# One transformer block, attention loop: GpSimd's stores, loads, table steps and splits in units of their own, and keys split over all tokens

## The chip, the cores and the metric

One core of a Trainium2 chip runs the whole program. The metric is device time in microseconds. The profile counts from the first to the last instruction (the span); the time of an execution is a little longer than its span. The engines are TensorE (PE, with its weight loads PEld), VectorE (DVE), ScalarE (ACT), GpSimd (POOL) and SyncE (SP, which issues transfers).

## The reference, cut to what matters

One layer of a diffusion backbone over 1024 latent tokens and 256 context tokens, width 1024, in float32. Tokens are normalised and modulated, projected, mixed by a pooling mixer (half the width) and by neighbourhood attention (8 heads of 64), projected out, and sent through a squared-ReLU MLP. The part that the change touches is the attention:

```python
s_loc = einsum('bnqhd,brnkhd->bhnqrk', q_r, k_b) * scale      # keys of the window
s_loc = where(col_mask, s_loc + bias, -inf)                    # learned 2-D position bias
s_ctx = einsum('bnqhd,bkhd->bhnqk', q_r, k_ctx) * scale        # all 256 context keys
p = softmax(concatenate([s_loc, s_ctx]))
o = p_loc @ v_b + p_ctx @ v_ctx
```

The latent grid has 16 rows of 64 columns. Each query sees a window of 8 rows by 16 columns and all context keys. After it come `mix @ w_out`, a gate row (`gt1`), the residual, and the second modulation (`sc2`, `sh2`).

## The kernel before, in words

**Three passes.** A float32 product is made of three products on rounded parts. A "split" makes them: `hi` is a cast of the source to the rounded type, `lo = src - hi`; then `hi*hi + hi*lo + lo*hi` is accumulated. A split of 128x512 is two instructions. `split` (L156) casts on ScalarE (L146) and subtracts on VectorE (L152). In the attention `high` (L1112) casts on ScalarE and puts the subtraction into the list `lows`, which `low()` empties on VectorE. `parts_of` with an engine (L901, L902) does both on GpSimd.

**Units.** Tokens are regrouped into 8 bands of 8 columns (128 tokens each). The attention runs over 32 units: 4 pairs of heads `j`, 8 bands `m` each. A unit's 128 queries see three bands of local keys (m-1, m, m+1) and the context; the bands 0 and 7 see two. A software pipeline runs over units, `for i in range(N + 4)` with N = 32. Iteration i does, among others:

- `weighed(i - 4)`: the weighted output of unit i-4 into the head page `heads[j]` (VectorE);
- `scores(i)` (L991): scores of both heads on TensorE into PSUM `S`; then on VectorE the bias table is added and the minimum `nm` found (L1027); between the two heads `share(i - 1)`: reciprocal of the sums `ri` on VectorE (L1042) and its copy over 128 columns `rb` on GpSimd (L1044);
- `turn(i - 2)`: TensorE transposes `rb` and the probabilities (L1057); `fifth_kept`: ScalarE copies them (`px`, L1071); `turn_kept`: ScalarE and VectorE copy the rest (`pt`, L1076);
- `exps(i, e)`: exponentials and sums on ScalarE (L1038);
- `values(i - 3)`: probabilities times values on TensorE (`pa`, L1091).

There are two `S` buffers, one for each head, so the scores of unit i+1 wait for VectorE's pass over unit i. Two output products of the query projection, `last_query("P4", i)`, stand in iterations 0 and 1. In iterations 32 to 35 the first products of the output projection (`pox`) take the scores' place.

**Order.** `in_order` ties each engine's instructions to the order in which the program writes them, for TensorE, ScalarE, VectorE and SyncE in the loop and for GpSimd through `first_pool`. An instruction that waits holds up everything behind it on its engine.

**What else stands in the loop.** Each of these is placed by hand at an iteration:

- bias tables: `tables(j)` (L867) loads the raw table of head pair j (SyncE) and then subtracts it from the mask in four steps of three GpSimd instructions (L884). There are two table pairs; j uses pair `j % 2`. Before, one step is taken at the top of each iteration from m = 1 on.
- splits of keys and queries: each half of 512 tokens of a head pair is split by itself, so `keys[j, b]` has b = 0, 1. The units m = 3 and m = 4 see bands of both halves, and their local scores are computed in two pieces.
- modulation rows: the gate row "a" and the rows "sc" and "sh" are summed over partitions by eight small matmuls (L236), copied or gated, stored to DRAM by four DMAs of GpSimd (`mod_out`, L253), and "sc" and "sh" are loaded back as columns (L623). `column_sums` (L620) does all of that in one go, at iterations 5 and 8; row "a" is gated and stored at iteration 4. All stand ahead of `scores(i)`, so ahead of `rb` on GpSimd.
- accumulating DMAs of GpSimd (`add_to`, L187): second halves of the heads at i = 3 mod 8 (from 11), first halves at i = 15, 23, 31.
- the output projection's weights: `weight_load` at the iterations in `LOADS` (SyncE), `weight_split(n)` at those in `HALVES`; `mixed_split(j)`, the split of the finished head page's first half, at iterations 8, 16, 24 and 32.

**Memory.** Most tiles are pages of 128x1024 from a pool of 33 (`page`); eight more tiles of that size lie in the pool `whl` (called `small` or `spare` below). A tile takes a buffer when one is free; whoever writes it first waits until the last reader of the buffer's former tile is done.

Of the kernel before, what the change touches and what calls it, by code (L numbers as in the profile page):

```python
# [18 lines left out]
P = 128  # L19
# [61 lines left out]
def hybrid_block(ctx, tc, x, ctx_in, w_mod, b_mod, gp1, gp2, w_in, pool_w, rpb, w_out, w1, w2, vectors,  # L81
# [189 lines left out]
    with tc.tile_pool(name="ps1", bufs=6, space=PSUM) as ps1, tc.tile_pool(name="tmp1", bufs=3) as tmp:  # L271
# [348 lines left out]
        def column_sums(name, acc, to, bank):  # L620
            nc.scalar.copy(acc[:, :256], mod_sums_of(name, acc, bank))
            mod_out(name, acc)
            nc.gpsimd.dma_start(to, gates[name].rearrange("o (k p) -> p (o k)", p=P))  # L623
# [267 lines left out]
        keys, queries, kcs = {}, {}, []  # L891

        def parts_of(to, j, b, small=False, engine=None):
            name = f"{'k' if to is keys else 'q'}P{j}_{b}"
            src = kT[j][:, b * 512 : (b + 1) * 512] if to is keys else qT[j][b]
            t = whl.tile([P, 1024], F32R, tag="hl", name=name) if small else page(name, F32R)
            hi, lo = to[j, b] = t[:, :512], t[:, 512:]
            if engine is None:
                split(src, hi, lo)
            else:  # L900
                engine.tensor_copy(hi, src)  # L901
                engine.tensor_tensor(lo, src, hi.bitcast(F32), sub)  # L902
# [42 lines left out]
        with in_order(ET.PE, ET.Pool, ET.Activation, ET.DVE, ET.SP) as pooling:  # L945
            banks = {of: [bank(f"p{of}{j}") for j in range(2)] for of in "KQ"}
            use(-1)
            for step, (n, of, j) in enumerate([(n, of, j) for n, of in products for j in range(2)]):
# [23 lines left out]
                if step == 20:  # L972
                    parts_of(keys, 0, 0)
                if step == 22:
                    parts_of(queries, 0, 0, True)


    with (
# [12 lines left out]
        def scores(i):  # L991
# [4 lines left out]
            q = queries[j, m // 4]  # L996
# [4 lines left out]
            t0, t1 = (m - 1, m + 2) if inner else (m + o - 1, m + o + 1)  # L1001
            at = 128 if inner else 256
# [37 lines left out]
        def share(i):  # L1040
# [3 lines left out]
            nc.gpsimd.tensor_copy(shares[i].rearrange("p (e t) -> p e t", e=2),  # L1044
                                  ri.rearrange("p (e o) -> p e o", o=1).to_broadcast([P, 2, HD]))
# [74 lines left out]
        def mixed_split(j):  # L1120
            mp = mix["A12"][j] = page(f"mix0_{4 + j}", F32R)
            high(heads[j][:, :512], mp[:, :512], mp[:, 512:])

        def weight_split(n):
# [911 lines left out]
```

## Time and profile before

| | us |
|---|---|
| time, median of 3 runs | 1037.98 |
| lowest and highest | 1036.62, 1038.22 |
| profiled execution, its own time | 1037.68 |
| span of that execution | 1035.9 |
| mean granted TensorE clock | 0.995 |
| attention loop's scores, first and last start | 218.95, 324.81 |

The profile is read by stage: TensorE's busy time in a stretch, and where it is idle, which engine's instruction released it. Busy time of TensorE is modelled, so the starts of successive units are a better measure of a unit's length than busy time is. Engines off the path may be idle at no cost.

### The profile page before, as it was taken

The page shows a single profiled execution, that of the slowest core. Times are in us where ns is not written, and L with a number is a line of the kernel's source. Part 1 is how long each engine was busy: PE and PEld are TensorE (multiplying, and loading weights), DVE is VectorE, ACT ScalarE, POOL GpSimd, SP SyncE. Part 2 cuts the span into 40 slices and gives each one's busy share as a digit, 9 for nine tenths or more (in the row PEclk, how much of TensorE's full clock was granted, in tenths as well). Part 3 has the DMA queues.
Part 4 walks back from the last instruction along what each step waited for, and adds up shares of the span by engine and source line. Part 5 has one row for each costly group of instructions (what it writes and reads, how often), then busy time and mean ns, then how long its engine had stood idle before and what let it go on. Part 6 is the DMA issues. An engine that isn't in the chain of part 4 may idle for free.

```text
span 1035.9 us, 16106 instructions
## 1 busy us (share of the span) xinstructions
PE 1015.6 (98%) x5958; PEld 842.6 (81%) x5958; DVE 752.6 (73%) x1165; ACT 549.0 (53%) x951; POOL 133.0 (13%) x214
## 2 busy tenths in 40 slices
PE   8999999998999999999999999999999999999997
PEld 6788888876888888888888888888888888888885
DVE  5588757875886598878998888755766666547576
ACT  7573255355898556876655544555543334334431
POOL 3011200245732312310000000000000000000001
PEclk9999999998999999999999999999999999999999
DMA  9999798542338786794786666536967766656556
GB/s 342 330 257 333 255 265 282 203 102 63 73 74 214 175 193 193 231 265 165 250 274 208 221 199 229 203 112 240 324 230 268 246 226 220 203 175 195 171 182 212
DMA packets 123134, 222.71 MB, mean 215 GB/s; under 512 B 9456, under 2 KB 55152, under 8 KB 123056
## 3 DMA queue, kind: packets, MB, share of 16 engines
q1 hardware_dynamic: 96560, 171.14, 50.5%
q0 software_dynamic: 9360, 19.58, 9.3%
q10 hardware_dynamic: 17136, 30.97, 8.0%
q8 instruction: 47, 0.77, 0.3%
q14 instruction: 31, 0.25, 0.1%
HBM read 168.16 MB, written 52.45 MB: 213 GB/s over the span
## 4 chain that ended last, share of the span: by engine, by line
PE 73%; ACT 1%; issue 1%; DVE 0%; POOL 0%; DMA 0%; POOLq 0%; DVEq 0%; ACTq 0%
PE phz L198 3%; PE phv L198 3%; PE phx L198 3%; PE pyx L198 3%; PE pa L1091 3%; PE phx L199 3%; PE pyx L200 3%; PE phx L200 3%; PE pyv L199 3%; PE phz L200 3%; PE pyz L199 3%; PE pyx L199 3%; PE phv L200 3%; PE pyz L198 3%; PE pyv L198 3%; PE phv L199 3%
## 5 line engine op out<-in xcount | busy, mean ns | idle before, releaser
L1038 ACT ACTIVATE sp<-sp,nm 128x640 f32<-128x640 f32 (+1 forms) x64 | 51.6, 806 | 9.3 <-DVE ri L1042 4.5
L1622 ACT ACTIVATE c<-c 128x512 f32<-128x512 f32 x48 | 30.3, 632 | 44.3 <-DVE c L1742 25.1
L1027 DVE CUSTOM_DVE_ANT_0 sp<-S,tab 128x640 f32<-128x640 f32 (+1 forms) x56 | 44.5, 794 | 12.7 <-PE pz L1057 6.8
L146 ACT CAST wpS<-S 128x512 fp32r<-128x512 f32 x64 | 38.7, 616 | 28.1 <-PE phv L200 10.1
L198 PE MATMUL phx<-thB,wpA 128*128 128x512 f32 x128 | 50.2, 392 | 0.0
L199 PE MATMUL phx<-tlB,wpA 128*128 128x512 f32 x128 | 49.9, 390 | 0.0
L200 PE MATMUL phx<-thB,wpA 128*128 128x512 f32 x128 | 49.9, 389 | 0.0
L152 DVE TENSOR_TENSOR wpS<-S,wpS 128x512 fp32r<-128x512 f32 x64 | 43.4, 686 | 8.2 <-ACT wpS L146 8.2
L140 POOL TENSOR_TENSOR ry<-vy,nhalf 128x1 f32<-128x1 f32 x8 | 5.9, 740 | 280.7 <-DVE vy L138 280.7
L1623 ACT ACTIVATE c<-c 128x512 f32<-128x512 f32 x48 | 30.2, 630 | 14.4 <-DVE sa L1705 13.6
L1076 DVE COPY pt<-T 128x512 f32<-128x512 f32 x32 | 22.0, 687 | 9.7 <-PE T L1057 6.8
L198 PEld LDWEIGHTS phx<-thB,wpA 128*128 128x128 f32 x128 | 24.0, 188 | 5.5 <-ACT s L1673 0.5
L1091 PE MATMUL pa<-pt,v 128*64 128x128 f32 x352 | 26.5, 285 | 1.6 <-ACT px L1071 1.4
L200 PEld LDWEIGHTS phx<-thB,wpA 128*128 128x128 f32 x128 | 24.0, 188 | 5.0
L199 PEld LDWEIGHTS phx<-tlB,wpA 128*128 128x128 f32 x128 | 24.1, 188 | 4.8
L1012 PE MATMUL S<-kP,qP 64*128 64x256 f32 (+2 forms) x240 | 25.8, 324 | 0.9 <-DVE nm L1027 0.9
L198 PE MATMUL phz<-thB,wpS 128*128 128x512 f32 x64 | 25.0, 391 | 0.0
L198 PE MATMUL phv<-thT,wpA 128*128 128x512 f32 x64 | 25.0, 391 | 0.0
L200 PE MATMUL phz<-thB,wpS 128*128 128x512 f32 x64 | 24.9, 390 | 0.0
L199 PE MATMUL phv<-tlT,wpA 128*128 128x512 f32 x64 | 24.9, 389 | 0.0
L199 PE MATMUL phy<-tlT,wpS 128*128 128x512 f32 x64 | 24.9, 389 | 0.0
L198 PE MATMUL phz<-thT,wpS 128*128 128x512 f32 x64 | 24.9, 389 | 0.0
(1112 smaller groups left out, 3419.2 us busy)
## 6 DMA issues: line engine op xcount, KB each, us to landing
b<-in_w SPq DMA_DIRECT2D x64, 512.0 KB, 4.4
hrS<-hdS SPq DMA_DIRECT2D x32, 512.0 KB, 5.1
hrA<-hdA SPq DMA_DIRECT2D x24, 512.0 KB, 5.5
wm<-in_w_mod SPq DMA_DIRECT2D x16, 512.0 KB, 9.8
wa_0w<-in_w SPq DMA_DIRECT2D x16, 512.0 KB, 4.8
wa_1w<-in_w SPq DMA_DIRECT2D x16, 512.0 KB, 4.5
hdA<-c ACTq DMA_DIRECT2D x32, 256.0 KB, 2.7
hdS<-sa ACTq DMA_DIRECT2D x32, 256.0 KB, 2.4
```

The source lines that it names most:

```text
L146: nc.scalar.copy(hi, src)
L152: nc.vector.tensor_tensor(lo, src, hi.bitcast(F32), sub)
L198: nc.tensor.matmul(ps, ahi, bhi, start=first, stop=False, skip_group_check=more)
L199: nc.tensor.matmul(ps, ahi, blo, start=False, stop=False, skip_group_check=more)
L200: nc.tensor.matmul(ps, alo, bhi, start=False, stop=last, skip_group_check=more)
L1012: nc.tensor.matmul(S[e][:, c0 : c0 + k[0].shape[1]], q[n_q][hs, cols], k[n_k][hs], start=(n_q + n_k == 0), stop=(n_q == 1))
L1027: nc.vector.tensor_tensor_reduce(out=to, in0=s, in1=bt, scale=1.0, scalar=BIG, op0=add, op1=ALU.min, accum_out=nm)
L1038: nc.scalar.activation(sp, sp, AF.Exp, bias=least[i, e], scale=-1.0, accum_out=sums[i][:, e : e + 1])
L1076: copy(turns[i].rearrange("p e i t -> p (e i) t")[:, :, h * HD : (h + 1) * HD], turned[i][h].rearrange("p (a t) -> p a t", a=8))
L1091: nc.tensor.matmul(pa[e * HD : (e + 1) * HD, cols], v[:, f : f + HD], turns[i][:, e, c] if c < 4 else fifths[i][:, :, (e + 1) * HD : (e + ...
L1622: nc.scalar.activation(r, src, AF.Relu)
L1623: nc.scalar.activation(r, r, AF.Square)
```

## The change

GpSimd's other work in the loop is written as a table `jobs`, which names for an iteration what is issued right behind `scores(i)`, so behind that iteration's `rb`.

- `column_sums` only sums and copies; the store (`out_of`) and the load as a column (`columns_of`) become jobs: row "a" stored in unit 5, "sc" stored in 6 and loaded in 10, "sh" stored in 9 and loaded in 12.
- Table steps (`built`) become jobs: pair 1 in units 0 to 4, pair 2 in 9, 10, 12, 13 (two steps), pair 3 in 18, 20 (two), 21 (two). The first of each only loads.
- `mixed_split` of head pairs 0 to 2 and the first four weight halves go from ScalarE and VectorE to GpSimd: units 8, 16, 24 and 26, 28, 29, 30 (before: 8, 16, 24 and 12, 14, 20, 22). The weight loads move from 8, 16 to 16, 20.
- Keys are split into one `hi` and one `lo` tile over all 1024 tokens of a head pair (`key_parts`), so that every unit takes its local keys as one slice. The halves are still written one by one. The second half of pair 2 goes from GpSimd (iteration 7) to ScalarE and VectorE (unit 0). GpSimd's other splits of keys and queries move from 6, 8, 9, 14, 15, 16 to 7, 14, 17, 18, 22, 25. Which tiles lie in pages and which in `whl` changes.
- The last unit's `rb` copy goes from GpSimd to VectorE.

```diff
-        def column_sums(name, acc, to, bank):
+        def column_sums(name, acc, bank):
             nc.scalar.copy(acc[:, :256], mod_sums_of(name, acc, bank))
-            mod_out(name, acc)
+
+        def columns_of(name, to):
             nc.gpsimd.dma_start(to, gates[name].rearrange("o (k p) -> p (o k)", p=P))
...
-        keys, queries, kcs = {}, {}, []
+        kparts, qparts, kcs = [None] * 4, {}, []
+
+        def apart(src, hi, lo, pool):
+            if pool:
+                nc.gpsimd.tensor_copy(hi, src)
+                nc.gpsimd.tensor_tensor(lo, src, hi.bitcast(F32), sub)
+            else:
                 split(src, hi, lo)
+
+        def part_page(name, spare):
+            return whl.tile([P, 1024], F32R, tag="hl", name=name) if spare else page(name, F32R)
+
+        def key_parts(j, b, spare=False, pool=False):
+            if kparts[j] is None:
+                kparts[j] = [part_page(f"kP{j}{n}", spare) for n in "hl"]
+            bs = slice(b * 512, b * 512 + 512)
+            apart(kT[j][:, bs], kparts[j][0][:, bs], kparts[j][1][:, bs], pool)
+
+        def query_parts(j, b, spare=False, pool=False):
+            t = part_page(f"qP{j}_{b}", spare)
+            qparts[j, b] = t[:, :512], t[:, 512:]
+            apart(qT[j][b], *qparts[j, b], pool)
...
                 if step == 20:
-                    parts_of(keys, 0, 0)
+                    key_parts(0, 0)
                 if step == 22:
-                    parts_of(queries, 0, 0, True)
+                    query_parts(0, 0, True)
...
-            local = []
-            for b in range(2):
-                b0, b1 = max(t0, 4 * b), min(t1, 4 * b + 4)
-                if b0 < b1:
-                    local.append((at + (b0 - t0) * P, [a[:, (b0 - 4 * b) * P : (b1 - 4 * b) * P] for a in keys[j, b]]))
-            parts = local + [(512, ck)] if inner else [(0, ck)] + local
+            ts = slice((m - 1) * P, (m + 2) * P) if inner else slice((m + o - 1) * P, (m + o + 1) * P)
+            local = [a[:, ts] for a in kparts[j]]
+            parts = ((128, local), (512, ck)) if inner else ((0, ck), (256, local))
...
-            nc.gpsimd.tensor_copy(shares[i].rearrange("p (e t) -> p e t", e=2),
-                                  ri.rearrange("p (e o) -> p e o", o=1).to_broadcast([P, 2, HD]))
+            (nc.gpsimd if i < N - 1 else nc.vector).tensor_copy(
+                shares[i].rearrange("p (e t) -> p e t", e=2),
+                ri.rearrange("p (e o) -> p e o", o=1).to_broadcast([P, 2, HD]))
...
-        LOADS, HALVES = (8, 16, 26, 28), (12, 14, 20, 22, 32, 33, 33, 34)
+        LOADS, HALVES = (16, 20, 26, 28), (None, None, None, None, 32, 33, 33, 34)
...
-        def high(src, hi, lo):
+        def high(src, hi, lo, pool=False):
+            if pool:
+                apart(src, hi, lo, True)
+                return
             nc.scalar.copy(hi, src)
             lows.append(lambda: nc.vector.tensor_tensor(lo, src, hi.bitcast(F32), sub))
...
-            early_parts = [(keys, 0, 1, True), (keys, 1, 0, True), (queries, 1, 0, True), (keys, 1, 1),
-                           (keys, 2, 0, True), (queries, 2, 0, True)]
-            for p in early_parts[:3]:
-                parts_of(*p)
-            for j in range(2):
-                last_query("P7", j)
-                for p in early_parts[3 + 2 * j : 5 + 2 * j]:
-                    parts_of(*p)
-            parts_at = {1: (queries, 0, 1)}
-            parts_at.update({i: (to, j, b, j == 2, nc.gpsimd) for i, to, j, b in
-                             ((6, queries, 1, 1), (7, keys, 2, 1), (8, queries, 2, 1), (9, keys, 3, 0),
-                              (14, keys, 3, 1), (15, queries, 3, 0), (16, queries, 3, 1))})
-            coming_tables = iter(())
+            key_parts(0, 1)
+            key_parts(1, 0, True)
+            query_parts(1, 0, True)
+            last_query("P7", 0)
+            key_parts(1, 1)
+            last_query("P7", 1)
+            key_parts(2, 0, True)
+            query_parts(2, 0)
+
+            table = [None] + [tables(j) for j in (1, 2, 3)]
+            built = lambda j: next(table[j])
+            out_of = lambda n: mod_out(n, accs[n])
+            jobs = {0: [(built, 1), (key_parts, 2, 1)], 1: [(built, 1)], 2: [(built, 1)], 3: [(built, 1)], 4: [(built, 1)],
+                    5: [(out_of, "a")], 6: [(out_of, "sc")], 7: [(query_parts, 1, 1, True, True)],
+                    8: [(mixed_split, 0, True)], 9: [(built, 2), (out_of, "sh")],
+                    10: [(columns_of, "sc", scale2), (built, 2)], 12: [(columns_of, "sh", s2), (built, 2)],
+                    13: [(built, 2), (built, 2)], 14: [(query_parts, 3, 0, False, True)],
+                    16: [(mixed_split, 1, True)], 17: [(query_parts, 2, 1, True, True)],
+                    18: [(built, 3), (key_parts, 3, 0, False, True)], 20: [(built, 3), (built, 3)],
+                    21: [(built, 3), (built, 3)], 22: [(key_parts, 3, 1, False, True)], 24: [(mixed_split, 2, True)],
+                    25: [(query_parts, 3, 1, False, True)], 26: [(weight_split, 0, True)], 28: [(weight_split, 1, True)],
+                    29: [(weight_split, 2, True)], 30: [(weight_split, 3, True)]}
             for i in range(N + 4):
-                if i < N and units[i][1] == 1 and units[i][0] < 3:
-                    coming_tables = tables(units[i][0] + 1)
-                next(coming_tables, None)
...
                     mod_gate("a", accs["a"], gain, rest_of_bank)
-                    mod_out("a", accs["a"])
...
-                    column_sums("sc", accs["sc"], scale2, rest_of_bank)
+                    column_sums("sc", accs["sc"], rest_of_bank)
...
-                    column_sums("sh", accs["sh"], s2, rest_of_bank)
+                    column_sums("sh", accs["sh"], rest_of_bank)
...
-                if i > 0 and i % 8 == 0:
-                    mixed_split(i // 8 - 1)
+                if i == N:
+                    mixed_split(3)
...
                     scores(i)
+                    for f, *args in jobs.get(i, ()):
+                        f(*args)
...
-                if i in parts_at:
-                    parts_of(*parts_at[i])
+                if i == 1:
+                    query_parts(0, 1)
```

More of the change, by code (lines that the diff above doesn't have):

```diff
@@ L1118, in low, with mixed_split, weight_split @@
                 lows.pop(0)()
-        def mixed_split(j):
+        def mixed_split(j, pool=False):
             mp = mix["A12"][j] = page(f"mix0_{4 + j}", F32R)
-            high(heads[j][:, :512], mp[:, :512], mp[:, 512:])
-        def weight_split(n):
+            high(heads[j][:, :512], mp[:, :512], mp[:, 512:], pool)
+        def weight_split(n, pool=False):
             kk, cs = kks[n // 2], slice(n % 2 * 512, n % 2 * 512 + 512)
@@ L1128, in weight_split @@
             hi, lo = wo[kk]
-            high(raw_o[0, kk][:, cs], hi[:, cs], lo[:, cs])
+            high(raw_o[0, kk][:, cs], hi[:, cs], lo[:, cs], pool)
         def weight_load(h, kk):
```

13 lines of the change are left out of this document (1 added, 12 removed).

## The prediction

> **What bounds the kernel now.** I read the page first, then busy time by stage, then TensorE's and GpSimd's instructions inside the slow stage. Page:
>
> ```profile
> span 1035.9 us, 16106 instructions
> PE 1015.6 (98%) x5958; PEld 842.6 (81%) x5958; DVE 752.6 (73%) x1165; ACT 549.0 (53%) x951; POOL 133.0 (13%) x214
> ```
>
> TensorE is the bound: 98% busy over the span. What a change can win lies where TensorE stands still or does more than it must. The stages (columns: stretch, then busy us and instruction count of PE, PEld, DVE, ACT, POOL, then granted clock, DMA share, GB/s):
>
> ```profile
> 219.00:328.00 109.00, 101.56 (x1667) 89.88 (x1667) 84.14 (x232) 86.13 (x229) 54.46 (x109) 0.97 0.42 106
> 328.00:420.00 92.00, 91.84 (x493) 75.61 (x492) 65.74 (x102) 54.85 (x101) 19.65 (x24) 1.00 0.76 190
> 480.00:740.00 260.00, 259.99 (x1151) 214.45 (x1151) 206.97 (x313) 137.15 (x229) 3.50 (x6) 1.00 0.66 218
> ```
>
> The change edits the attention loop, 219 to 328 us. There TensorE is idle for 7.44 us and its clock is granted at 0.97; what follows is full. A microsecond won in the loop therefore reaches the end, as long as the stage behind it finds its weights. TensorE's rows in time order (start, duration, engine, line, operands; in brackets the idle time before and its releaser). `S` is the start of a unit's scores, `rb` the transposes that need GpSimd's copy of the reciprocal sums:
>
> ```profile
> 240.28 0.80 PE L1012 MATMUL S<-kP,qP 64*128 64x384 f32 x6
> 244.41 0.37 PE L1057 MATMUL pa<-ident,rb 64*128 64x64 f32 x1 [2.98 <-POOL rb L1044]
> 252.62 0.39 PE L1012 MATMUL S<-kch,qP 64*128 64x256 f32 x2
> 255.45 0.81 PE L1012 MATMUL S<-kP,qP 64*128 64x384 f32 x6
> 258.70 0.27 PE L1057 MATMUL pa<-ident,rb 64*128 64x64 f32 x1 [2.10 <-POOL rb L1044]
> ```
>
> These are units 6, 8 and 9. Two gaps, 2.98 and 2.10 us, both waiting for `rb`. GpSimd's queue says why `rb` is late, and the row of DMA issues how long a store takes to land (last column, us):
>
> ```profile
> 238.44 1.95 POOL L253 DMA_DIRECT2D gsc<-accsc  x4 [0.58 <-ACT accsc L621]
> 243.12 0.94 POOL L623 DMA_DIRECT2D sc<-gsc  x1 [2.72 <-DVE nm L1027]
> 244.05 0.53 POOL L1044 COPY rb<-ri 128x128 f32<-128x128 f32 x2
> 257.42 0.93 POOL L623 DMA_DIRECT2D s<-gsh  x1 [2.04 <-DMA gsh<-accsh]
> gsc<-accsc POOLq DMA_DIRECT2D x4, 1.0 KB, 2.8
> ```
>
> Four stores of a row to DRAM (1.95 us of issue), and right behind them, in the same unit, the load of that row as a column, which must wait until the stores have landed: 2.72 us here, 2.04 us the second time. (The first is named after VectorE; 238.44 + 1.95 + 2.8 = 243.2 says that it was the landing.) Two `rb` copies come out together at 244.05: one unit's had been held up. The gap costs more than itself, as the granted clock shows (third column from the right):
>
> ```profile
> 244.00:246.00 2.00, 1.59 (x24) 1.47 (x26) 0.03 (x1) 0.97 (x3) 1.91 (x5) 0.50 0.12 2
> 256.00:258.00 2.00, 0.61 (x10) 0.40 (x6) 1.92 (x5) 0.43 (x2) 0.58 (x1) 1.00 0.00 0
> ```
>
> After the gap of 2.98 us TensorE runs at half clock; the gap of 2.10 us left it at 1.00.
>
> [...] The rows put the fall right behind the gap, so I count it with the gap.
>
> **The change, part by part.**
>
> *Stores and column loads in units of their own* (row "a" in unit 5; "sc" stored in 6, loaded in 10; "sh" 9 and 12; each behind that unit's `rb`). A column load now stands three units or more behind its stores, some 9 us against a landing of 2.8. To price units without such waits I take the last head pair, units 24 to 31:
>
> ```profile
> 252.05 0.64 PE L236 MATMUL pz<-accsh,ones 128*32 128x256 f32 x8
> 279.10 0.55 PE L1012 MATMUL S<-kch,qP 64*128 64x256 f32 x2
> 303.96 0.39 PE L1012 MATMUL S<-kch,qP 64*128 64x256 f32 x2
> 321.81 0.80 PE L1012 MATMUL S<-kP,qP 64*128 64x384 f32 x6
> 324.81 0.39 PE L1012 MATMUL S<-kch,qP 64*128 64x256 f32 x2
> 327.66 0.50 PE L198 MATMUL pox<-wo_0h,mix 128*128 128x512 f32 x1
> ```
>
> They are the row products ahead of unit 8's scores, units 16, 24, 30, 31 and the first output product. An inner unit takes 324.81 - 321.81 = 3.00, an edge unit 327.66 - 324.81 = 2.85. Units 6 and 7 took 252.62 - 240.28 = 12.34; without the wait they take 3.00 + 2.85, plus the eight row products, which stay: 252.62 - 252.05 = 0.57. That is 6.42. **First term 5.92.** Its lower bound is the gap alone, 2.98.
>
> The head pair of units 24 to 31 takes 327.66 - 303.96 = 23.70 in all. Units 8 to 15 took 279.10 - 252.62 = 26.48, an excess of 2.78, of which at least 2.10 is the second `rb` gap. **Second term 2.78**, lower bound 2.10; the rest belongs to the next edit.
>
> *Splits of the mixed operand and of the first four weight halves go from ScalarE and VectorE to GpSimd* (seven splits: three in units 8 to 15, three in 16 to 23, one in unit 24). Units 16 to 23 took 303.96 - 279.10 = 24.86, 1.16 over the last head pair. **Third term 1.16.** The shape of it, in one unit with a split:
>
> ```profile
> 268.68 0.88 PE L1091 MATMUL pa<-pt,v 128*64 128x128 f32 x12 [0.23 <-ACT px L1071]
> ```
>
> TensorE waits for the fifth chunk's copy behind ScalarE's extra 0.6 us. If the score-to-minimum chain were to refill such gaps, the term would be 0: its lower bound. The last head pair holds one such split itself, which I do not price.
>
> What GpSimd takes over, by its own rows (`rb`, a split's two halves, three table steps), and VectorE's low half without and with a GpSimd split under way:
>
> ```profile
> 275.16 0.29 POOL L1044 COPY rb<-ri 128x128 f32<-128x128 f32 x1 [2.70 <-DVE ri L1042]
> 275.40 0.61 POOL L901 CAST kP<-kT 128x512 fp32r<-128x512 f32 x1
> 276.10 1.29 POOL L902 TENSOR_TENSOR kP<-kT,kP 128x512 fp32r<-128x512 f32 x1
> 225.26 1.28 POOL L884 TENSOR_TENSOR tab<-msk,U 128x128 f32<-128x128 f32 x3
> 270.32 0.68 DVE L1114 TENSOR_TENSOR wo_0l<-wor,wo_0h 128x512 fp32r<-128x512 f32 x1
> 276.66 1.27 DVE L1114 TENSOR_TENSOR wo_0l<-wor,wo_0h 128x512 fp32r<-128x512 f32 x1
> ```
>
> `rb` and a split end 276.10 + 1.29 - 275.16 = 2.23 us after they begin; `rb` and two table steps take 0.29 + 2 x 1.28 = 2.85; a store 0.29 + 1.95 = 2.24; a column load with a table step 0.29 + 0.94 + 1.28 = 2.51. All are under the 3.00 of a unit, so the next `rb` isn't late, and GpSimd's extra work costs nothing. The cover is the unit's length and then one unit more (an `rb` is used in the unit after the one that makes it); without it each split would cost TensorE up to 1.9 us. The accumulating DMAs of units 11, 15, 19, 23, 27 and 31 stay there, and no job was put into those units; units 1 and 2 keep theirs beside a table step, as before.
>
> The row at 276.66 shows VectorE's low half stretched from 0.68 to 1.27 while GpSimd subtracts. [...]
>
> *Keys split over all tokens.* Units m = 3 and m = 4 of each head pair took their local keys in two pieces, 18 score matmuls instead of 12; now in one piece:
>
> ```profile
> 309.83 0.80 PE L1012 MATMUL S<-kP,qP 64*128 64x384 f32 x6
> 310.81 0.22 PE L1057 MATMUL pa<-ident,rb 64*128 64x64 f32 x1
> 312.48 1.00 PE L1012 MATMUL S<-kP,qP 64*128 64x256 f32 x11
> 313.73 0.21 PE L1057 MATMUL pa<-ident,rb 64*128 64x64 f32 x1
> 315.63 0.96 PE L1012 MATMUL S<-kP,qP 64*128 64x128 f32 x12
> 316.79 0.21 PE L1057 MATMUL pa<-ident,rb 64*128 64x64 f32 x1
> ```
>
> Scores of m = 2 last 310.81 - 309.83 = 0.98, of m = 3 1.25, of m = 4 1.16: 0.27 and 0.18 saved. Four head pairs: **fourth term 1.80.** It holds while TensorE sets the unit; if the minimum of the scores sets it, it is 0, the lower bound. Pair 0's and pair 3's whole keys fill two pages each, pair 1's and pair 2's lie in the pool of eight; the pages held when the loop starts are as many as before.
>
> *The second key half of pair 2 goes to ScalarE and VectorE in unit 0*, a split of 0.61 and 0.68:
>
> ```profile
> 222.94 0.69 DVE L937 TENSOR_TENSOR q<-pqv,q 128x512 f32<-128x512 f32 x1 [0.35 <-PE pqv L200]
> 224.03 0.82 DVE L1027 CUSTOM_DVE_ANT_0 sp<-S,tab 128x640 f32<-128x640 f32 x1 [0.39 <-PE S L1012]
> ```
>
> VectorE idles 0.35 + 0.39 = 0.74 just there, in wait for TensorE. Cost 0; 0.7 if that cover is missed. *The last `rb` on VectorE* and *the later weight loads* lie beside output products and cost 0: the first weight half is split in unit 26, ten units after its load.
>
> **Sum.** 5.92 + 2.78 + 1.16 + 1.80 = 11.66. The span of 1035.9 becomes 1024.2; the profiled execution took 1037.68, 1.78 around the span, so 1026.0. That execution is 0.30 under the median of 1037.98, hence **1026.3** on the scale of the runs shown. All lower bounds: 2.98 + 2.10 + 0 + 0 - 0.7 = 4.4, or 1033.6. The upper: of the 7.44 us of idle time the two gaps are 5.08 and the third term at most 1.16; the 1.2 left could go too, if the new order of splits frees VectorE in units 2 and 3 and the one split not priced counts: 12.9, or 1025.1.
>
> **Rivals.**
>
> 1. *One gap stays* (0.16). The pages are tighter from unit 18 on: raw weights now live to units 28 and 30. If a GpSimd job waits for a page, `rb` behind it is late, and a 3 us gap with its slow clock comes back: 11.66 - 5.92 = 5.74 saved, 1032.2. For: SyncE's loads wait for pages in this loop already. Against: pair 3's key pages, now taken in unit 18, were taken in units 9 and 14 before, and a job waits only for what is older than itself.
> 2. *Only the stores pay* (0.10): scores are paced by VectorE's minimum, and terms three and four vanish. Saved 5.92 + 2.78 = 8.70, 1029.3. Against: in the last head pair m = 3 and 4 take longer than their neighbours though ScalarE splits nothing there.
> 3. *Slower: the next weights come late* (0.06). Held pages delay the first loads for the output projection, which GpSimd then accumulates onto:
>
> ```profile
> to_1w<-in_w_out POOLq DMA_DIRECT2D x1, 512.0 KB, 10.4
> 345.89 1.05 ACT L146 CAST to_0h<-to_0w 128x1024 fp32r<-128x1024 f32 x1
> ```
>
> That accumulation begins about when the loop ends (327.66) and needs 10.4, ready near 338; the split that wants it starts at 345.89. So lateness up to 8 us is free and counts in full beyond. It is slower than now from 8 + 11.7 = 20 us, which is seven units; at 24 us, 1042. Against: pages come free with each of the last units.
> 4. *No change* (0.04): the loop ends earlier and the output stage waits by as much, for transfers that don't move with it: 1038. Against: those loads are released by TensorE's own progress, and TensorE there idles 0.16 us of 92.
>
> **How the numbers follow.** The forecast has 0.64 and its own range is 1025.1 to 1028.5. With rivals 2 and 1 (to 1032.2) 0.90 lies inside; the outer range is 1024.6 to 1032.4, a little beyond the upper estimate on the fast side. About 0.2% (2 us) is what a measurement of this kernel can tell from no change. Faster: 0.64 + 0.16 + 0.10 = 0.90; same 0.04; slower 0.06.
>
> **What would show it.** Right: no `rb` idle over 1 us on TensorE, granted clock 1.00 from 240 to 252, scores of m = 3 and 4 lasting 0.98, 192 instead of 240 key matmuls, head pairs of about 23.2 us, and the first output product near 316. Wrong: GpSimd jobs with a wait before them and `rb` pairs coming out together; ScalarE still ahead of the `pa` products; VectorE's minima stretched beyond 0.82 beside GpSimd; idle time on TensorE behind 328 that is not there now.

## The result and the profile after

The changed kernel takes 1030.3 us (median of 6 runs, 1029.43 to 1031.4) against 1038.03 for the kernel before in the same comparison. The ratio is 0.993, with a 95% interval of 0.9917 to 0.9943. The forecast was 1026.3 with a range of 1024.6 to 1032.4: the kernel got faster as forecast, the time lies inside this range but outside the forecast's own (1025.1 to 1028.5), and 4.0 us of the forecast gain of 11.7 are missing.

The profiled execution of the changed kernel took 1031.34, 1.0 above its median; why is told under the second experiment. Its page:

```profile
span 1029.6 us, 16022 instructions
PE 1014.6 (99%) x5910; PEld 840.7 (82%) x5910; DVE 747.1 (73%) x1160; ACT 546.8 (53%) x945; POOL 142.6 (14%) x225
```

The 48 fewer matmuls are those of the key pieces. The stages of the changed kernel (columns as in the prediction; the last three rows stand around the first units of the loop):

```profile
219.00:328.00 109.00, 106.14 (x1684) 92.97 (x1683) 85.82 (x239) 89.66 (x236) 67.26 (x120) 0.98 0.44 109
328.00:420.00 92.00, 91.39 (x457) 74.90 (x456) 68.53 (x105) 55.81 (x103) 18.60 (x22) 1.00 0.76 194
...
222.00:224.00 2.00, 1.49 (x4) 1.20 (x5) 2.00 (x4) 0.87 (x2) 0.00 (x0) 0.68 0.75 211
224.00:226.00 2.00, 2.00 (x6) 1.51 (x6) 2.00 (x7) 0.50 (x1) 0.00 (x0) 0.50 0.02 5
226.00:228.00 2.00, 2.00 (x17) 1.53 (x15) 1.37 (x4) 1.02 (x4) 0.00 (x0) 0.97 0.00 0
```

TensorE is idle for 2.86 us in the stretch of the loop (109.00 - 106.14) where it was idle for 7.44, yet its clock still averages 0.98: the half clock has moved from 244 to 223. TensorE's rows of the changed kernel in time order:

```profile
210.69 0.39 PE L198 MATMUL pqv<-S3h,wQT3h 128*128 128x512 f32 x1
...
216.90 0.50 PE L198 MATMUL pK<-hx,wKT4h 128*128 128x512 f32 x1 [0.60 <-DVE kT L946]
...
220.80 0.39 PE L1018 MATMUL S<-kch,qP 64*128 64x256 f32 x2 [0.88 <-DVE kT L948]
...
222.51 0.63 PE L198 MATMUL pqv<-hx,wQT4h 128*128 128x512 f32 x1 [0.72 <-DVE q L946]
...
227.05 0.44 PE L1018 MATMUL S<-kP0h,qP 64*128 64x384 f32 x2
...
244.10 0.44 PE L1018 MATMUL S<-kP0h,qP 64*128 64x384 f32 x2
...
250.52 0.38 PE L1018 MATMUL S<-kch,qP 64*128 64x256 f32 x2
...
263.41 0.27 PE L1064 MATMUL pa<-ident,rb 64*128 64x64 f32 x1 [0.34 <-POOL rb L1050]
...
274.31 0.38 PE L1018 MATMUL S<-kch,qP 64*128 64x256 f32 x2
...
297.55 0.39 PE L1018 MATMUL S<-kch,qP 64*128 64x256 f32 x2
...
320.78 0.50 PE L198 MATMUL pox<-wo_0h,mix 128*128 128x512 f32 x1
```

These are the starts of units 0 (220.80), 1 (227.05), 6 (244.10), 8 (250.52), 16, 24 and the first output product. Both old gaps of 2.98 and 2.10 us are gone; 0.34 is left of the second kind. New are the three gaps at the top. Stretch by stretch, as differences of such starts (us won against before, negative where lost; the last column is the fifth experiment's kernel, told below):

| stretch | before lasted | forecast won | the change won | e5 won |
|---|---|---|---|---|
| up to the first score | 218.95 | 0 | -1.85 | -0.54 |
| units 0 to 5 | 21.33 | 0.45 | -1.97 | 0.33 |
| units 6 and 7 | 12.34 | 5.92 | 5.92 | 5.94 |
| units 8 to 15 | 26.48 | 2.78 + 0.45 | 2.69 | 3.25 |
| units 16 to 23 | 24.86 | 1.16 + 0.45 | 1.62 | 1.65 |
| units 24 to 31 | 23.70 | 0.45 | 0.47 | 0.52 |

Units 6 and 7 and units 16 to 31 went as forecast. What is missing was lost before unit 2, and a little in units 8 to 15. The first row holds differences between executions too: the kernel of e3 (one of the experiments below), unchanged up to there, starts its first score at 219.68, 0.73 later than the kernel before, and the three profiled executions with the change's program up to there (the change, e2, e4) start it between 220.80 and 221.57. The first loss has its cause in the view of waits for the 17 us before the loop (205 to 222 us; engine, what it writes and line, releaser: us in total, times, longest):

```profile
ACT kP0h L146 <- DVE kT L948: 8.7, 1, 8.7
DVE kP0l L152 <- PE pqv L200: 8.2, 1, 8.2
```

VectorE's subtraction `kP0l`, the low part of the first half of pair 0's keys, doesn't wait for its operands: what releases it is a product of the queries (`pqv`), which has nothing to do with keys. It waits for a page, as I read it; e1 and e8 test that. VectorE's rows for this piece, first in the kernel before, then in the changed kernel:

```profile
206.06 0.75 DVE L152 TENSOR_TENSOR kP<-kT,kP 128x512 fp32r<-128x512 f32 x1
...
214.35 0.69 DVE L152 TENSOR_TENSOR kP0l<-kT,kP0h 128x512 fp32r<-128x512 f32 x1 [8.21 <-PE pqv L200]
```

Before the change the first key half took one page (`hi` and `lo` side by side); now the first half asks for two at once, and by a count of the program's allotments only one is free at that place. The other comes free with the products of query projection P7. The order of TensorE's instructions gave way to that: those products now start at 210.69, ahead of the second half of the last key product (216.90), where before they came behind it (TensorE's timeline of the kernel before):

```profile
213.19 0.39 PE L200 MATMUL pK<-hx,wKT4l 128*128 128x512 f32 x1
213.42 0.39 PE L198 MATMUL pqv<-S3h,wQT3h 128*128 128x512 f32 x1
```

So the second half of the keys comes last, and unit 0 starts with all that hangs on it: the keys' second half, its splits, and the queries behind them on VectorE. TensorE idles 0.60, 0.88 and 0.72 us, and in this execution the clock falls to 0.50 behind them.

The second loss is on GpSimd's queue, units 9 to 12 of the changed kernel:

```profile
258.45 0.29 POOL L1050 COPY rb<-ri 128x128 f32<-128x128 f32 x1 [0.42 <-DVE ri L1048]
259.07 0.94 POOL L624 DMA_DIRECT2D sc<-gsc  x1 [0.33 <-issue]
260.03 1.27 POOL L885 TENSOR_TENSOR tab<-msk,U 128x128 f32<-128x128 f32 x3
261.25 0.91 POOL L188 DMA_DIRECT2D y<-f  x1
261.88 1.18 POOL L188 DMA_DIRECT2D ss<-f  x1
262.43 0.92 POOL L1050 COPY rb<-ri 128x128 f32<-128x128 f32 x1
```

The column load and the table step of unit 10 end at 261.30, and right behind them stand unit 11's two accumulating DMAs, which are issued ahead of its `rb`. That `rb` therefore has no idle time before it, and TensorE waits 0.34 us for it at 263.41. (It also lasts 0.92 instead of 0.29 behind these DMAs, but it does so in e5 as well, where no wait is left.)

### The profile page after: what moved, and what is told of

The parts are those of the page before. It is cut to its first block, busy times and chain, and to the rows that moved or that the text cites. A ratio compares the mean times of both kernels' runs of the same rounds, so it can differ in the third digit from the quotient of the medians.

```text
span 1029.6 us, 16022 instructions
## 1 busy us (share of the span) xinstructions
PE 1014.6 (99%) x5910; PEld 840.7 (82%) x5910; DVE 747.1 (73%) x1160; ACT 546.8 (53%) x945; POOL 142.6 (14%) x225
## 4 chain that ended last, share of the span: by engine, by line
PE 94%; DMA 2%; DVE 1%; issue 0%; ACT 0%; POOL 0%; SPq 0%; DVEq 0%; POOLq 0%; ACTq 0%
PE pu L449 4%; PE pa L1098 4%; PE S L1018 3%; PE phz L198 3%; PE phv L198 3%; PE phx L198 3%; PE pyx L198 3%; PE phx L200 3%; PE pyx L200 3%; PE phz L200 3%; PE pyx L199 3%; PE pyv L198 3%; PE pyz L199 3%; PE pyv L199 3%; PE phv L200 3%; PE pyz L198 3%
## 5 line engine op out<-in xcount | busy, mean ns | idle before, releaser
L199 PE MATMUL phz<-tlB,wpS 128*128 128x512 f32 x64 | 24.9, 390 | 0.0
L200 PE MATMUL phy<-thT,wpS 128*128 128x512 f32 x64 | 24.9, 389 | 0.0
```

Source lines behind the costliest of these rows:

```text
L199: nc.tensor.matmul(ps, ahi, blo, start=False, stop=False, skip_group_check=more)
L200: nc.tensor.matmul(ps, alo, bhi, start=False, stop=last, skip_group_check=more)
```

## The experiments

| | us | ratio to before, 95% interval |
|---|---|---|
| e1: pair 0's whole keys in the pool of eight | 1027.14 | 0.9895 [0.9882, 0.9909] |
| e2: second key half of pair 2 back on GpSimd | 1030.09 | 0.9927 [0.9914, 0.9941] |
| e3: before, with stores and loads moved alone | 1032.24 | 0.9945 [0.9933, 0.9958] |
| e4: the change, splits back | 1033.37 | 0.9957 [0.9944, 0.9969] |
| e5: e1, column loads moved on | 1026.33 | 0.9886 [0.9871, 0.9902] |
| e6: e1, keys in two pieces | 1028.0 | 0.9902 [0.9888, 0.9916] |
| e7: e5, a query split on GpSimd | 1026.45 | 0.9889 [0.9875, 0.9903] |
| e8: before, with two pages for the first key half | 1040.48 | 1.0022 [1.0013, 1.0031] |

The kernel before ran beside them at 1038.08 and 1038.1.

**e1: is it the pages?** The first key half is taken where the program allots from the pool of eight, and the queries' tiles move to pages in exchange.

```diff
                 if step == 20:
-                    key_parts(0, 0)
+                    query_parts(0, 0)
                 if step == 22:
-                    query_parts(0, 0, True)
+                    key_parts(0, 0, True)
...
-            query_parts(1, 0, True)
+            query_parts(1, 0)
```

> The changed kernel, but pair 0's two key tiles are taken in step 22 from the pool of eight, its first query half in step 20 in one page, and pair 1's first query half in a page; nothing else. Theory A (two pages are wanted in step 20 and only one is free, so VectorE waits 8.21 us for the other, the query product P7 is put ahead of a key product, and the loop starts late and cold): TensorE's products stand in the order of before, VectorE's wait is gone, the first scores start near 219 instead of 220.8, unit 0 takes 3.9 instead of 6.25 us, and the time falls from 1030.3 to about 1026. Theory B (VectorE is late because it got pair 2's second key half in unit 0): the time stays within 1 us of 1030.3.

It took 1027.14, 3.2 less than the change and 1.1 above what was expected; most of that rest is the second loss, which e1 still has. The low half runs with no wait, both halves of it together (VectorE's timeline of e1):

```profile
213.73 1.47 DVE L152 TENSOR_TENSOR kP0l<-kT,kP0h 128x512 fp32r<-128x512 f32 x2
```

and the clock stays up (stretch of e1):

```profile
224.00:226.00 2.00, 2.00 (x18) 1.64 (x15) 1.61 (x5) 0.31 (x1) 0.21 (x1) 1.00 0.38 69
```

The first score starts at 219.74 instead of 220.80, unit 1 follows 3.89 us later instead of 6.25 (before: 3.88), and only the gaps of unit 3 and a 0.38 at unit 12 are left. The pages are the first loss; e8 shows it from the other side.

**e2: or the split that moved into unit 0?** The second key half of pair 2, which the change put on ScalarE and VectorE there, goes to GpSimd in unit 6.

```diff
-            jobs = {0: [(built, 1), (key_parts, 2, 1)], 1: [(built, 1)], 2: [(built, 1)], 3: [(built, 1)], 4: [(built, 1)],
-                    5: [(out_of, "a")], 6: [(out_of, "sc")], 7: [(query_parts, 1, 1, True, True)],
+            jobs = {0: [(built, 1)], 1: [(built, 1)], 2: [(built, 1)], 3: [(built, 1)], 4: [(built, 1)],
+                    5: [(out_of, "a")], 6: [(out_of, "sc"), (key_parts, 2, 1, False, True)], 7: [(query_parts, 1, 1, True, True)],
```

> The changed kernel, but pair 2's second key half is split by GpSimd in unit 6 instead of by ScalarE and VectorE in unit 0. Theory A (pages): VectorE's wait of 8 us before the loop stays, and so does the time, 1030.3 within 1 us. Theory B (the extra split on VectorE): the loop's first units get 2 to 4 us shorter, 1026 to 1028.

1030.09: nothing changed, and the wait of 8.2 us on `kP0l` stands in its trace as it does in that of the change. That split costs nothing, as the prediction had it. The run showed something else. Its three gaps ahead of and in unit 0 are the same to 0.01 us (0.60, 0.87, 0.73), but the clock does not fall (stretches of e2):

```profile
222.00:224.00 2.00, 1.27 (x7) 1.02 (x6) 2.00 (x5) 0.65 (x2) 0.00 (x0) 1.00 0.78 226
224.00:226.00 2.00, 2.00 (x10) 1.34 (x8) 2.00 (x5) 0.20 (x1) 0.00 (x0) 1.00 0.04 9
```

Units 0 and 1 take 4.72 and 4.63 here, 9.35 together, against 6.25 + 4.00 = 10.25 in the profiled execution of the change. The half clock in that execution is thus worth 0.9 us, about the distance between it and the median. Of the change's six executions the two longest, 1031.34 and 1031.4, have a mean granted clock of 0.996, the other four (1029.43 to 1030.3) 0.998 or 0.999. The price of the pages without it is 1.4 us in these two units (9.35 against 3.89 + 4.05 in e1) and 1.36 in a later start (221.10 against 219.74, of which some tenths are the execution), 2.8 in all; by the medians e2 stands 2.95 over e1.

**e3: the stores and column loads alone.** From the kernel before: row "a" stored in unit 5, "sc" in 6, "sh" in 9, each behind `scores(i)`, and loaded as columns in 10 and 12; all else as it was.

```diff
-        def column_sums(name, acc, to, bank):
+        def column_sums(name, acc, bank):
             nc.scalar.copy(acc[:, :256], mod_sums_of(name, acc, bank))
-            mod_out(name, acc)
+
+        def columns_of(name, to):
             nc.gpsimd.dma_start(to, gates[name].rearrange("o (k p) -> p (o k)", p=P))
...
+            jobs = {5: [(out_of, "a")], 6: [(out_of, "sc")], 9: [(out_of, "sh")],
+                    10: [(columns_of, "sc", scale2)], 12: [(columns_of, "sh", s2)]}
...
                     scores(i)
+                    for f, *args in jobs.get(i, ()):
+                        f(*args)
```

> The kernel before with one edit: the stores and column loads in units 5, 6, 9, 10 and 12, behind that unit's scores. If the gaps at units 6 and 9 and the slow clock behind the first come from the column load's wait for its stores: both gaps go, 5.9 + 2.3 us are won, about 1029.8. If the clock had fallen anyway: 2.98 + 2.1 us, about 1033. If the wait only moves to another unit: no change, 1038.

1032.24, a gain of 5.8, 2.4 short of the expected 1029.8. Units 6 and 7 take 6.42 as in the change, and the old gaps are gone. But two new ones stand in units 11 and 12 (TensorE's timeline of e3):

```profile
258.45 0.27 PE L1058 MATMUL pa<-ident,rb 64*128 64x64 f32 x1 [1.15 <-POOL rb L1045]
...
262.68 0.27 PE L1058 MATMUL pa<-ident,rb 64*128 64x64 f32 x1 [1.07 <-POOL rb L1045]
```

and GpSimd's timeline of e3 shows why, here for the first:

```profile
253.00 1.96 POOL L253 DMA_DIRECT2D gsh<-accsh  x4 [0.23 <-issue]
254.95 0.62 POOL L902 CAST kP<-kT 128x512 fp32r<-128x512 f32 x1
255.66 1.28 POOL L903 TENSOR_TENSOR kP<-kT,kP 128x512 fp32r<-128x512 f32 x1
256.91 1.25 POOL L885 TENSOR_TENSOR tab<-msk,U 128x128 f32<-128x128 f32 x3
258.10 0.29 POOL L1045 COPY rb<-ri 128x128 f32<-128x128 f32 x1
```

The store of unit 9 has a key split and a table step behind it, 5.16 us of work without a break (253.00 to 258.16) between two `rb`. The second is the queue of the change's second loss: from 258.10 on `rb`, the column load of "sc", a table step and unit 11's two accumulating DMAs stand without a break, and the next `rb` starts at 261.68. With a store that no longer waits for its landing, the queue is late by its own length. The first two terms of the sum need more than the move of the stores: the table steps and splits around unit 9 must be spread as well, and the change does that.

**e4: the splits back on ScalarE and VectorE.** From the change: the splits of the mixed operand and of the first four weight halves, and the weight loads, as before.

```diff
-        LOADS, HALVES = (16, 20, 26, 28), (None, None, None, None, 32, 33, 33, 34)
+        LOADS, HALVES = (8, 16, 26, 28), (12, 14, 20, 22, 32, 33, 33, 34)
...
-                if i == N:
-                    mixed_split(3)
+                if i > 0 and i % 8 == 0:
+                    mixed_split(i // 8 - 1)
```

and the jobs `mixed_split` and `weight_split` taken out of units 8, 16, 24, 26, 28, 29 and 30.

> The changed kernel with the splits of the mixed operand and of the first weight halves back on ScalarE and VectorE at their old units, and the weight loads too. If those splits held TensorE up: 1.2 to 1.6 us slower than the changed kernel, about 1031.8. If the units have room for them on ScalarE and VectorE: the same, 1030.3.

1033.37: 3.1 us slower than the change, about twice what was expected. Five units wait for ScalarE's copy of the fifth chunk; the first and the last of them in TensorE's timeline of e4:

```profile
270.48 0.88 PE L1098 MATMUL pa<-pt,v 128*64 128x128 f32 x12 [0.28 <-ACT px L1078]
...
301.58 0.88 PE L1098 MATMUL pa<-pt,v 128*64 128x128 f32 x12 [0.35 <-ACT px L1078]
```

The gap names only part of the price. The units that it falls in (14, 16, 20, 22, 24) last 3.35, 3.55, 3.45, 3.35 and 3.56, against 3.00, 2.83, 3.02, 3.00 and 2.83 in the change: 2.6 in all, where the five gaps of 0.28 to 0.39 sum to 1.66. Another 0.5 stands in the scores of units 16 and 24, which last 1.06 there instead of 0.82; where the rest comes from I have not shown.

**e5: the second loss.** From e1: the column load of "sc" goes from unit 10 to 12, that of "sh" from 12 to 15, so that no column load stands with a table step in unit 10, right ahead of unit 11's accumulating DMAs.

```diff
-                    10: [(columns_of, "sc", scale2), (built, 2)], 12: [(columns_of, "sh", s2), (built, 2)],
-                    13: [(built, 2), (built, 2)], 14: [(query_parts, 3, 0, False, True)],
+                    10: [(built, 2)], 12: [(columns_of, "sc", scale2), (built, 2)],
+                    13: [(built, 2), (built, 2)], 14: [(query_parts, 3, 0, False, True)], 15: [(columns_of, "sh", s2)],
```

> e1_key0_late with the column load of row sc moved from unit 10 to 12 and that of row sh from 12 to 15. If the idle time before unit 10's transposes (0.38 us in e1_key0_late, waiting for GpSimd's rb) comes from a column load and a table step in unit 10 followed by unit 11's two accumulating DMAs: it goes, unit 12 takes 3.0 instead of 3.6 us, and the time is 0.4 to 0.6 below e1_key0_late, about 1026.6. If it comes from the accumulating DMAs alone: unchanged, 1027.1.

1026.33, 0.8 less than e1 by medians of four executions each, whose ranges just meet (1026.52 the lowest of e1, 1026.66 the highest of e5). By starts unit 12 takes 3.01 instead of 3.61 and the loop is 0.57 shorter, which is what was expected; the rest is not shown to be the edit's. GpSimd's timeline of e5 around unit 11:

```profile
255.07 1.26 POOL L885 TENSOR_TENSOR tab<-msk,U 128x128 f32<-128x128 f32 x3
256.52 0.90 POOL L188 DMA_DIRECT2D y<-f  x1 [0.18 <-issue]
257.13 1.19 POOL L188 DMA_DIRECT2D ss<-f  x1
257.70 0.92 POOL L1050 COPY rb<-ri 128x128 f32<-128x128 f32 x1
```

The DMAs now have an idle moment before them, `rb` follows the DMAs as it must, and no `rb` gap is left on TensorE. The whole loop in one stretch, from the first score to the first output product:

```profile
219.49:316.51 97.02, 96.17 (x1618) 85.58 (x1617) 78.94 (x225) 83.17 (x222) 65.97 (x120) 1.00 0.43 105
```

97.02 against 327.66 - 218.95 = 108.71 before: 11.69 less, where the four terms of the prediction sum to 11.66. This kernel is faster than both the kernel before and the change: its interval lies below that of the change (0.9917 to 0.9943).

**e6: what the whole keys are worth.** From e1: `hi` and `lo` stay whole, but the scores of m = 3 and m = 4 take them in two pieces again, cut at token 512.

```diff
-            ts = slice((m - 1) * P, (m + 2) * P) if inner else slice((m + o - 1) * P, (m + o + 1) * P)
-            local = [a[:, ts] for a in kparts[j]]
-            parts = ((128, local), (512, ck)) if inner else ((0, ck), (256, local))
+            t0, t1 = (m - 1, m + 2) if inner else (m + o - 1, m + o + 1)
+            at = 128 if inner else 256
+            local = []
+            for b in range(2):
+                b0, b1 = max(t0, 4 * b), min(t1, 4 * b + 4)
+                if b0 < b1:
+                    local.append((at + (b0 - t0) * P, [a[:, b0 * P : b1 * P] for a in kparts[j]]))
+            parts = local + [(512, ck)] if inner else [(0, ck)] + local
```

> e1_key0_late with the local scores of m = 3 and m = 4 taken in two pieces again, from the whole key tiles. By the prediction's fourth term it is 1.8 us slower, 1028.9. By the measured unit lengths (m = 3 now 3.00 where 2.88 was forecast, since VectorE's pass over the scores then sets the unit) it is 4 x (0.15 + 0.17) = 1.3 us slower, 1028.4. If VectorE's pass sets both units: the same, 1027.1.

1028.0, 0.9 over e1, less than either price expected. By starts of units, m = 3 and m = 4 of the last head pair take 3.15 + 3.17 against 3.01 + 2.99 in e1, 0.32 more; pairs 0 and 2 show 0.33 and 0.35, pair 1 nothing, because the 0.38 at unit 12 of e1 doesn't appear in e6: as I read it, the slower unit 11 gives GpSimd the time that it lacked. So whole keys are worth 0.33 per head pair and 1.3 in all where no `rb` is late, not 0.45 and 1.80.

**e7: the last wait in the loop.** From e5: the split of pair 0's second query half goes from ScalarE and VectorE to GpSimd in unit 1, to free VectorE in units 1 to 3; of pair 1's table steps the one of unit 1 goes to unit 5.

```diff
-            jobs = {0: [(built, 1), (key_parts, 2, 1)], 1: [(built, 1)], 2: [(built, 1)], 3: [(built, 1)], 4: [(built, 1)],
-                    5: [(out_of, "a")], 6: [(out_of, "sc")], 7: [(query_parts, 1, 1, True, True)],
+            jobs = {0: [(built, 1), (key_parts, 2, 1)], 1: [(query_parts, 0, 1, False, True)], 2: [(built, 1)], 3: [(built, 1)], 4: [(built, 1)],
+                    5: [(out_of, "a"), (built, 1)], 6: [(out_of, "sc")], 7: [(query_parts, 1, 1, True, True)],
...
-                if i == 1:
-                    query_parts(0, 1)
```

> e5_columns_moved with pair 0's second query half split by GpSimd in unit 1 instead of by ScalarE and VectorE, and the table steps of pair 1 one unit later. If TensorE's wait at unit 3 (0.48 + 0.37 us, for VectorE's minimum of unit 2) comes from the VectorE half of that split just ahead of it: about 0.6 to 0.8 us less than e5_columns_moved, near 1026. If it comes from the product's own end: unchanged.

1026.45, no difference to e5 that can be told: the hoped-for 0.6 to 0.8 did not come. The two waits for `nm` at unit 3 (0.48 and 0.37 in e5) are there at 0.37 and 0.36. VectorE's timeline of e7 shows that it had been waiting itself just before:

```profile
228.46 0.82 DVE L1033 CUSTOM_DVE_ANT_0 sp<-S,tab 128x640 f32<-128x640 f32 x1 [0.40 <-PE pz L1064]
```

VectorE's other work there was not what held it. I read it as the chain from scores to minimum itself: `values` follows three units behind, so unit 2 has no value products yet to fill TensorE's time. No run here changes that.

**e8: the pages from the other side.** From the kernel before: only the low part of the first key half gets a page of its own; everything else stays.

```diff
-            hi, lo = to[j, b] = t[:, :512], t[:, 512:]
+            second = page(f"{name}l", F32R)[:, :512] if name == "kP0_0" else t[:, 512:]
+            hi, lo = to[j, b] = t[:, :512], second
```

> The kernel before with one edit: the low part of pair 0's first key half lies in a page of its own, so that step 20 takes two pages instead of one. Theory A (pages): VectorE waits some 8 us before the loop, the query product P7 comes ahead of a key product, the first units are late, and the time rises by 2 to 4 us, to 1040 to 1042. If the second page isn't the cause: 1038, unchanged.

1040.48: one page more makes the kernel before slower, and the wait appears in it with the same length (VectorE's timeline of e8):

```profile
214.48 0.69 DVE L152 TENSOR_TENSOR kP_0l<-kT,kP 128x512 fp32r<-128x512 f32 x1 [8.21 <-PE pqv L200]
```

The first score comes at 220.96 (2.01 later than before, 1.28 later than in e3), and units 0 and 1 take 4.72 + 4.63 against 3.88 + 4.06 (1.41 more): 2.7 to 3.4 us in all. In this execution, the fastest of e8's eleven, not all of that arrives at the end: units 6 and 7 took 9.39 us where they had taken 12.34, since the gap at unit 6 was there and the clock did not fall behind it. TensorE's row and the stretch behind it, in e8:

```profile
247.62 0.27 PE L1058 MATMUL pa<-ident,rb 64*128 64x64 f32 x1 [2.78 <-POOL rb L1045]
```

```profile
248.00:250.00 2.00, 2.00 (x42) 1.76 (x39) 0.82 (x2) 1.95 (x6) 1.62 (x2) 1.00 0.18 2
```

Units 9 and 10 lost part of that again: they take 6.48 + 3.11 instead of 5.20 + 2.66, because here the clock fell behind the second gap, where it had not in the kernel before (e8):

```profile
259.35 0.27 PE L1058 MATMUL pa<-ident,rb 64*128 64x64 f32 x1 [2.28 <-POOL rb L1045]
```

```profile
260.00:262.00 2.00, 2.00 (x23) 1.94 (x20) 0.69 (x1) 2.00 (x5) 2.00 (x3) 0.50 0.08 1
```

By starts the first output product is 329.88 - 327.66 = 2.2 later. Of the whole times, executions with the same mean granted clock are the fair pairs: at 0.997 the medians are 1039.63 and, before, 1036.65, at 0.995 they are 1040.92 and 1038.14, so 2.8 to 3.0 us for the page.

## Why the prediction was right or wrong

**First term, 5.92: right.** Units 6 and 7 were to take 3.00 + 2.85 + 0.57 = 6.42, and they take 250.52 - 244.10 = 6.42. e3 shows that moving the stores alone does it. That nearly half of the term was the clock and not the gap holds for these two units: with a gap of 2.78 and no fall of the clock they took 2.95 less in e8. It is not a fixed price of that gap, though: in e8 the fall came at the second gap, and units 6 to 10 together won 1.2, not 2.95.

**Second term, 2.78: right in size, with one condition not seen.** Units 8 to 15 won 2.69 with the fourth term's share in it, 3.25 in e5. e3 shows that it isn't the stores' move alone: without the spreading of table steps and splits 2.2 us come back as gaps of 1.15 and 1.07.

**Third term, 1.16: too small.** e4 puts the splits at 3.1 us by medians, 2.6 by the lengths of the units. Part of that lay in the kernel before, but not in this term. Units 12 and 14 with a split were 0.29 and 0.35 longer there than their equals without one, and that stood in the second term (the rest of 2.78 - 2.10 = 0.68 that the prediction left to this edit). And the yardstick, the last head pair, "holds one such split itself, which I do not price": unit 24 took 3.00 where unit 8 took 2.83, so 0.17 is missing for unit 24 and 0.17 for unit 16. That makes 1.16 + 0.64 + 0.34 = 2.1. In e4 unit 24 costs 0.73 instead of 0.17 and unit 20 0.43 instead of 0.29, while unit 12, held by a late `rb` in the change already, costs nothing more; why the first two cost more there no run shows. The lower bound of 0 is refuted: by e4 the score-to-minimum chain does not refill these gaps.

**Fourth term, 1.80: too large.** The scores of m = 3 do not last 0.98. TensorE and VectorE in the change, unit 27:

```profile
305.92 0.66 PE L1018 MATMUL S<-kP3h,qP 64*128 64x384 f32 x2
...
307.03 0.24 PE L1064 MATMUL pa<-ident,rb 64*128 64x64 f32 x1
```

```profile
305.27 0.80 DVE L1033 CUSTOM_DVE_ANT_0 sp<-S,tab 128x640 f32<-128x640 f32 x1
```

They last 307.03 - 305.92 = 1.11, since VectorE's pass over the second head of unit 26 ends only at 306.07 and holds that head's `S` buffer. That is the condition that the prediction named ("while TensorE sets the unit"); it fails for m = 3 by 0.13 and holds for m = 4. e6 has 0.33 per pair instead of 0.45. That the forecast time of the loop comes out to 0.03 us in e5 is therefore in part luck: the third term's shortfall and the fourth's excess cancel.

**The page sentence: wrong, 3.2 us.** "The pages held when the loop starts are as many as before" counts at one moment. The moment that counts is step 20, where `key_parts(0, 0)` takes both whole tiles while only half of the tokens are to be split. e1 takes the wait away and wins 3.2; e8 puts it into the kernel before and loses 2.8 to 3.0. The first rival had the mechanism, a page that comes late, but in the wrong place: it looked from unit 18 on and at GpSimd, whose jobs there have no wait before them, and it priced it at 5.9. That the time lies inside the stated range at all is therefore luck: the range was widened to 1032.4 for rivals 1 and 2, and neither took place as described.

**GpSimd's extra work at 0: nearly right, 0.6 to 0.8 us wrong.** The price of a column load with a table step, 2.51 with its `rb` and so under a unit's 3.00, was true: in the rows of the second loss they last 0.94 and 1.27. What failed is that "no job was put into those units" was taken to cover unit 11: its accumulating DMAs stand ahead of its `rb`, so unit 10's job has less than a unit. e5 moves that column load and wins 0.6 by starts, 0.8 by medians. By medians, 3.2 + 0.8 is the missing 4.0. Nor does the sum hold anything for VectorE beside a busier GpSimd, though one low half had lasted 1.27 instead of 0.68 in the kernel before: that 0 was an estimate, which no run tests alone. VectorE's 48 minima over 128x640 in the loop last 0.814 us in the mean in the change, as in the kernel before.

**What was set at 0 and held.** The second key half of pair 2 in unit 0 (e2: no difference), the last `rb` on VectorE, and the later weight loads: from the first output product to the end of the span it is 1029.6 - 320.78 = 708.8, where it was 1035.9 - 327.66 = 708.2. Rivals 3 and 4 put a loss of many us behind 328; it is 0.6, and this stretch is between 707.7 and 708.8 in all ten profiled executions. Rival 2's time, 1029.3, is near the result, but not its mechanism: e4 and e6 show that terms three and four pay.

## What to carry to other kernels

Count buffers at each place where the program allots them, in the order of allotment, and not at one later moment: a tile made larger to be read in one piece is held from its first half on (3.2 us in e1). Where orders are tied piece by piece, look at the other engines too: the late buffer here didn't just make VectorE wait 8.21 us, it put TensorE's query products (210.69) ahead of a key product (216.90), and the profile then named a releaser that has nothing to do with the data. On an engine whose instructions are tied in order, as GpSimd's are here, sum its work from one critical copy to the next, with what stands ahead of the next one, instead of holding each job against the length of a unit: in e3 5.16 us between two `rb` became 1.15 us of idle time on TensorE.

## What the hardware showed that was not expected

The granted clock does not follow the length of a gap alone. It fell to 0.50 with a single gap of 2.98 us in the kernel before (at 243.87, 0.54 before the end of the gap) and behind one of 2.28 in e8, and stayed at 1.00 after one of 2.78 in e8 and one of 2.10 in the kernel before. In the profiled execution of the change it fell after three gaps of 0.60, 0.88 and 0.72 within some 6 us; after the same three (0.60, 0.87, 0.73) in e2 it did not, and the two differ by 0.9 us in units 0 and 1. Once down, it was at 0.50 for 3.42 us in the change (222.72 to 226.14) and for 6.83 in the kernel before (243.87 to 250.70). In e8 it was about 3.4: the products at 260.06 take 1.55 instead of 0.88 and the scores at 262.39 take 1.24 instead of 0.80, while those at 263.47 take 0.28 again.

Idle time added up over some length does not part the cases either. The table takes 3.41 us, half of 6.83, back from the moment at which the clock fell, or, where it stayed up, back from the end of the last gap:

| execution | stretch, us | TensorE idle in it, us | clock behind it |
|---|---|---|---|
| before | 240.46 to 243.87 | 2.44 | 0.50 |
| before | 255.29 to 258.70 | 2.09 | 1.00 |
| e8 | 244.21 to 247.62 | 2.78 | 1.00 |
| e8 | 256.65 to 260.06 | 2.28 | 0.50 |
| the change | 219.31 to 222.72 | 1.60 | 0.50 |
| e2 | 219.40 to 222.81 | 1.60 | 1.00 |

The largest sum, 2.78, has no fall behind it, and 1.60 stands on both sides. What decides is not shown by these runs; busy time of TensorE is modelled, too.
